# A hybrid encoder block on one core: two weight sums made by adding transfers, the first feed-forward block prepared in the output projection, the product split in weight buffers

## The chip, the cores and the metric

The kernel runs on one core of one Trainium2 chip. The metric is the device time of one execution in microseconds (us); lower is better. The engines of the core are named as the profile names them: PE (matrix products; PEld its weight loads), DVE (vector work), ACT (activations and casts), POOL (a second, slower vector engine that also issues transfers), SP (issues transfers). Each engine takes its instructions in the order in which they stand in its own list, and waits on semaphores for what other engines or transfers must have done.

## The reference, cut to what matters

```
h = concat(meta, x)                          # 16 + 512 tokens, 1024 wide
p = rmsnorm(h) @ w_in                        # q,k,v of two attention branches, two gates
o_na, o_df = neighbourhood_attention(p) @ w_na_out, diff_attention(p) @ w_diff_out
x = x + (sigmoid(g_na) * o_na + sigmoid(g_df) * o_df) @ w_o
h = rmsnorm(x)
x = x + (silu(h @ w_gate) * (h @ w_up)) @ w_down        # w_gate, w_up: 1024 x 2816
return rmsnorm(x)[16:]
```

## The kernel before, in words

All data is float32. A product of two float32 operands is made of three products of operands that are each split in a high part (a cast by ACT) and a low part (source minus high part, by DVE): `mm3` issues hi·hi, hi·lo and lo·hi. So every weight block and every activation block goes once through ACT and once through DVE before PE can use it; `split` and `wsplit` do that. Activations lie transposed (channels on the 128 partitions, tokens along the row).

The program has these stages, one behind the other. **Prologue** (`setup`): SP loads the first weight block `wraw` in two halves and the eight rows `xr` of x; ACT and DVE split the first weight block, then scale and split each row into `xh` and `xl`; POOL issues the transfers of the vector `vec` (norm weights), of `lv` (the lambda vectors, repeated over all partitions) and of `mask`. The sum of squares `ssq` of the rows is made by ACT (squares) and DVE (adds); PE forms its mean (`ms`) between the products of the third weight block. **Attention** follows, with the input projection mixed into it. **Merge** (`pn`) and **output projection** (`po`, eight blocks m = 0 to 7 of 24 products): after each block DVE adds the product to the residual `m`, and `x_operands` makes from it the operands of the feed-forward products.

**Feed-forward**: 22 blocks f of 128 columns. Gate and up products of a block are made together by a scheme of seven half-size products in place of eight: `f_products` runs the products PB11, PT1, PT4, PT2, PB21, PB22 and PT3 of 12 matmuls of 256 columns each. Its weight operands are G (the gate block, two halves), up's second half, and four sums: up0+up1 (`W[:, 1]`), up0+up1+gate0 (PT2), gate0+up0 (PT3) and the sum of all four halves (PB22). Before the change `f_load` loads G, `W[:, 0]` (up's second half) and `V[:, 0]` (up's first half) by three transfers from SP, and `f_prep` makes the sums with three adds on DVE and splits everything. `f_load` runs two blocks ahead, `f_prep` one block ahead; for block 0, `f_load(0)` stands after m = 3 of the projection and `f_prep(0)` after m = 6. The squares of x for the second norm are summed by POOL (`sum_sq`), the last one by DVE. `glu` makes g[f] from the products. **Down projection** (`pdn`): the 22 tiles g are split into `gh` and `gl`, all in one loop behind the last feed-forward block, and `d_ahead` splits the pieces of w_down into `wring`. The last of eight output blocks is done in halves (`pdh`) with the final norm behind it.

The order on each engine's list is made by a scheduler from the order of the code, priorities and estimated waits; `tc.issue_after(x)` keeps what is inside it behind instruction x on the list.

Of the kernel before, what the change touches and what calls it, by code (L numbers as in the profile page):

```python
# [71 lines left out]
class Kernel:  # L72
# [34 lines left out]
    def wsplit(self, i, parts=1, eng=None):  # L107
# [5 lines left out]
        if eng is None:  # L113
            eng = nc.gpsimd if 3 <= i < 40 and i % POOL_MOD in POOL_SET else nc.vector
        h = nk // parts
        for k in range(0, nk, h):
            nc.scalar.copy(hi[:, k:k + h], raw[:, k:k + h])  # L117
# [35 lines left out]
    def split(self, hi, lo, src):  # L153
        self.nc.scalar.copy(hi, src)  # L154
        self.nc.vector.tensor_sub(lo, src, hi.bitcast(F32))  # L155
# [49 lines left out]
    def setup(self):  # L205
# [33 lines left out]
        self.wsplit(0, 2)  # L239
        for d in self.wload(1):  # L240
            d()
        self.wemit = 2
        for k in range(KT):
            nc.scalar.activation(self.xh[:, k], xr[k], AF.Copy, scale=self.g1[:, k:k + 1])  # L244
# [974 lines left out]
```

## Time and profile before

| | |
|---|---|
| median of 3 runs | 774.57 us (773.76 to 774.62) |
| the profiled execution | 773.11 us, span 771.3 us |
| mean granted TensorE clock | 0.986 |
| PE busy | 748.6 us, 97% of the span |
| DVE, ACT, POOL busy | 575.6, 379.7, 55.3 us |
| transfers | 87.88 MB, mean 114 GB/s |

The span is the time from the first to the last instruction of the profiled execution; 1.8 us of that execution lie outside it. In rows of instructions the columns are start, duration, engine, line, operation, out<-in with its shape, and in brackets how long the engine had been idle before and what ended that. Rows by stretches give for each stretch of the span its length, the busy time of each engine with its instructions, the granted clock of PE, the busy share of the transfer engines and GB/s. Durations of matmuls overlap, so the pace of PE is read from starts or from a stretch divided by its matmuls.

### The profile page before, as it was taken

How to read it: one execution, taken by the hardware profiler on the slowest of the kernel's cores; microseconds unless marked ns; L12 is line 12 of the kernel's file. 1: busy time of each engine (PE TensorE's matmuls, PEld its weight loads, DVE VectorE, ACT ScalarE, POOL GpSimd, SP SyncE). 2: the span in 40 equal slices, each digit the busy share in tenths (PEclk: the TensorE clock that was granted, in tenths of full speed). 3: DMA queues.
4: the chain of work that ended last, by engine and by line, in shares of the span. 5: the costliest groups of instructions: out<-in, count | busy, mean ns of one | idle time of the engine just before them, and what ended most of it. 6: DMA issues, size and time to landing. Idle time of an engine off the chain costs nothing.

```text
span 771.3 us, 12598 instructions
## 1 busy us (share of the span) xinstructions
PE 748.6 (97%) x4794; PEld 674.1 (87%) x4794; DVE 575.6 (75%) x1053; ACT 379.7 (49%) x669; POOL 55.3 (7%) x141
## 2 busy tenths in 40 slices
PE   7999999999999999999998999999999989999995
PEld 5899889998889888878887999999999987888884
DVE  5777897788788867648889899999999959632214
ACT  6345545545554546514554655555555556422201
POOL 2030110110011000001121000000000000000100
PEclk8999999999999999999998999999999999999998
DMA  7474643453563412235541333333333232633003
GB/s 261 136 182 143 158 123 103 123 152 104 137 159 101 121 58 80 82 110 163 169 132 42 110 110 110 110 107 104 104 104 108 66 102 68 206 103 95 1 1 109
DMA packets 34715, 87.88 MB, mean 114 GB/s; under 512 B 4512, under 2 KB 6576, under 8 KB 34656
## 3 DMA queue, kind: packets, MB, share of 16 engines
q1 hardware_dynamic: 32688, 82.97, 35.6%
q0 software_dynamic: 1136, 3.34, 1.5%
q8 instruction: 37, 0.61, 0.3%
q10 hardware_dynamic: 832, 0.79, 0.3%
q14 instruction: 22, 0.18, 0.1%
HBM read 70.01 MB, written 2.10 MB: 93 GB/s over the span
## 4 chain that ended last, share of the span: by engine, by line
PE 85%; DVE 9%; DMA 2%; issue 1%; ACT 1%; SPq 0%; DVEq 0%; ACTq 0%
PE pdn L144 4%; PE pdn L140 4%; PE pdn L142 4%; PE pa L140 4%; PE pa L144 4%; PE pb L140 4%; PE pg L140 4%; PE pa L142 4%; PE pb L142 4%; PE pb L144 4%; PE pg L144 4%; PE pg L142 4%; PE s L513 2%; PE pv L140 2%; PE pv L142 2%; PE pv L144 2%
## 5 line engine op out<-in xcount | busy, mean ns | idle before, releaser
L117 ACT CAST whi<-wraw 128x1024 fp32r<-128x1024 f32 (+1 forms) x57 | 58.9, 1033 | 56.9 <-PE pd L142 13.1
L118 DVE TENSOR_TENSOR wlo<-wraw,whi 128x1024 fp32r<-128x1024 f32 (+1 forms) x57 | 68.5, 1201 | 17.2 <-ACT whi L117 16.9
L144 PE MATMUL pdn<-gh,wring 128*128 128x512 f32 x138 | 53.8, 390 | 1.3 <-DVE wring L155 1.3
L140 PE MATMUL pdn<-gh,wring 128*128 128x512 f32 x138 | 53.8, 390 | 0.0
L142 PE MATMUL pdn<-gl,wring 128*128 128x512 f32 x138 | 53.7, 389 | 0.0
L140 PE MATMUL pg<-xh,whi 128*128 128x512 f32 x128 | 52.6, 411 | 0.4 <-DVE vt L379 0.4
L142 PE MATMUL pg<-xl,whi 128*128 128x512 f32 x128 | 50.6, 395 | 0.0
L144 PE MATMUL pg<-xh,wlo 128*128 128x512 f32 x128 | 50.2, 393 | 0.0
L155 DVE TENSOR_TENSOR wring<-draw,wring 128x1024 fp32r<-128x1024 f32 (+1 forms) x22 | 24.7, 1126 | 28.8 <-ACT wring L154 28.8
L154 ACT CAST wring<-draw 128x1024 fp32r<-128x1024 f32 (+1 forms) x22 | 21.0, 974 | 45.9 <-PE pdn L142 34.5
L154 ACT CAST fdh<-fG 128x1024 fp32r<-128x1024 f32 x22 | 23.2, 1056 | 36.8 <-PE pa L142 34.7
L154 ACT CAST ath<-tp 128x256 fp32r<-128x256 f32 (+1 forms) x48 | 20.5, 443 | 42.2 <-PE tp L637 22.0
L1137 POOL TENSOR_TENSOR ssq<-ssq,sq 128x512 f32<-128x512 f32 x11 | 16.4, 1493 | 345.6 <-ACT sq L1136 335.2
L155 DVE TENSOR_TENSOR wlo<-fG,whi 128x1024 fp32r<-128x1024 f32 x22 | 26.9, 1224 | 14.4 <-ACT whi L154 14.4
L517 ACT ACTIVATE e<-s,m 128x528 f32<-128x528 f32 x32 | 22.5, 704 | 23.0 <-DVE m L515 22.7
L144 PEld LDWEIGHTS pdn<-gh,wring 128*128 128x128 f32 x138 | 25.9, 188 | 7.1 <-DVE wring L155 1.7
L140 PE MATMUL pk<-xh,whi 128*128 128x256 f32 (+1 forms) x128 | 28.9, 303 | 3.1 <-ACT xh L244 3.1
L140 PEld LDWEIGHTS pdn<-gh,wring 128*128 128x128 f32 x138 | 25.9, 188 | 5.6 <-ACT wring L154 0.2
L142 PEld LDWEIGHTS pdn<-gl,wring 128*128 128x128 f32 x138 | 25.9, 188 | 5.3
L155 DVE TENSOR_TENSOR fwl<-fW,fwh 128x1024 fp32r<-128x1024 f32 x22 | 26.9, 1225 | 3.1 <-ACT fwh L154 3.1
L144 PEld LDWEIGHTS pg<-xh,wlo 128*128 128x128 f32 x128 | 24.0, 188 | 5.2
L621 ACT ACTIVATE en<-en,m 128x272 f32<-128x272 f32 x32 | 16.7, 522 | 24.1 <-DVE m L619 23.8
(292 smaller groups left out, 2596.2 us busy)
## 6 DMA issues: line engine op xcount, KB each, us to landing
wraw<-in_w_in_dram SPq DMA_DIRECT2D x39, 512.0 KB, 3.8
fG<-in_w_gate_dram SPq DMA_DIRECT2D x22, 512.0 KB, 3.5
kd<-khl SPq DMA_DIRECT2D x32, 264.0 KB, 4.2
draw<-in_w_down_dram SPq DMA_DIRECT2D x16, 512.0 KB, 3.6
fW<-in_w_up_dram SPq DMA_DIRECT2D x22, 256.0 KB, 2.6
fV<-in_w_up_dram SPq DMA_DIRECT2D x22, 256.0 KB, 2.9
qs<-qhl SPq DMA_DIRECT2D x32, 128.0 KB, 2.8
wraw<-in_w_o_dram SPq DMA_DIRECT2D x8, 512.0 KB, 3.5
```

What stands on the lines that cost most here:

```text
L117: nc.scalar.copy(hi[:, k:k + h], raw[:, k:k + h])
L118: eng.tensor_tensor(out=lo[:, k:k + h], in0=raw[:, k:k + h], in1=hi[:, k:k + h].bitcast(F32), op=ALU.subtract)
L140: nc.tensor.matmul(outs[i], wh, rhs[i][0], start=start, stop=False, **kw)
L142: nc.tensor.matmul(outs[i], wh, rhs[i][1], start=False, stop=False, **kw)
L144: nc.tensor.matmul(outs[i], wl, rhs[i][0], start=False, stop=stop, **kw)
L154: self.nc.scalar.copy(hi, src)
L155: self.nc.vector.tensor_sub(lo, src, hi.bitcast(F32))
L513: nc.tensor.matmul(sc[:, r0:r1], qs[:, q], kd[:, p, r0:r1], start=p == 0, stop=p == 1)
L517: nc.scalar.activation(e, sc, AF.Exp, bias=m, accum_out=l[:, c:c + 1])
L621: x = nc.scalar.activation(e[:, :n], e[:, :n], AF.Exp, bias=m, scale=-1.0, accum_out=l[:, 0:1])
L1137: (nc.gpsimd if m < n - 1 else nc.vector).tensor_tensor(out=ssq, in0=ssq, in1=sq, op=ALU.add)
```

## The change

1. **Prologue.** `wsplit(0, 2)` becomes a generator, and the split of the second weight half moves behind rows of x. The transfers of `lv` and `mask` go from POOL's queue to SP's, behind the two transfers of `rope`.
2. **Sums by adding transfers.** `f_load` loads up0 into `W[:, 1]` and gate0 into a new tile `D[:, 0]` as well as G and `W[:, 0]`, by four transfers from SP; then POOL issues two transfers that add up1 to `W[:, 1]` and up0 to `D[:, 0]` (`accum_op=ALU.add`). `f_prep` has two adds of 512 columns left (on `D[:, 1]`) in place of two of 512 and one of 1024. Each block now moves five quarter-megabyte plain pieces in place of four, and two adding ones.
3. **Block 0 in the projection.** `f_load(0)` stands ahead of the projection, and `f_prep(0)` is spread over m = 0, 1, 2 and 6. `f_load(1)` stands after m = 5. The sums of squares go to DVE, those of m = 4 to 7 behind the last operand of x; their mean on PE moves from the third product of block 0 to its last one, PT3.
4. **Product split in weight buffers.** The pool F of feed-forward weights stays open; the tiles `gh` take its buffers (`fW`, `fD`, `fwh`, ...) as they come free. Four of the splits stand ahead of the last `glu`, four behind the first two pieces of w_down, and the rest go four by four with the products. In the last feed-forward block PB21 goes ahead of PT2.

```diff
-        self.wsplit(0, 2)
         for d in self.wload(1):
             d()
         self.wemit = 2
+        first = self.wsplit(0, 2)
         for k in range(KT):
+            if k % 3 == 0:
+                next(first, None)
             nc.scalar.activation(self.xh[:, k], xr[k], AF.Copy, scale=self.g1[:, k:k + 1])
...
-        nc.gpsimd.dma_start(lv, a["lam"].partition_broadcast(P))
+        nc.sync.dma_start(lv, a["lam"].partition_broadcast(P))
...
-        nc.gpsimd.dma_start(self.mask, a["mask"])
+        nc.sync.dma_start(self.mask, a["mask"])
...
+            self.f_load(0)
+            prep = self.f_prep(0)
             for m in range(KT):
...
-                self.x_operands(XG, xbh, xbl, xg, x1, ng2, m)
-                self.sum_sq(bt, ssq, x1[:, m], m, KT)
-                if m == 3:
-                    self.f_load(0)
-                if m == 6:
-                    self.f_prep(0)
+                x = self.x_operands(XG, xbh, xbl, xg, x1, ng2, m)
+                last_x = getattr(x, "ins", x)
+                with tc.issue_after(last_x):
+                    if m < 4:
+                        self.sum_sq(bt, ssq, x1[:, m], m, nc.vector)
+                    if m < 3 or m == 6:
+                        next(prep, None)
+                if m == 5:
                     self.f_load(1)
+
+            with tc.issue_after(last_x):
+                for m in range(4, KT):
+                    self.sum_sq(bt, ssq, x1[:, m], m, nc.vector)
...
+            def split_g(n):
+                for k in range(len(gl), min(NF, len(gl) + n)):
+                    gh.append(next(place))
+                    gl.append(G.tile([P, T], F32R, name="gl", tag="g", bufs=NF + 1))
+                    self.split(gh[k], gl[k], g[k])
...
+                if f == NF - 1:
+                    split_g(4)
                 while held:
...
             self.d_ahead(2)
+            split_g(4)
             pd = {}
-            for k in range(NF):
-                gl.append(G.tile([P, T], F32R, name="gl", tag="g", bufs=NF + 1))
-                self.split(gh[k], gl[k], g[k])
...
+                if k % 4 == 0:
+                    split_g(4)
                 block(0, k)
                 block(1, k)
...
         W = F.tile([P, 2, 4, P], F32, name="fW", tag="fW", bufs=2)
-        nc.sync.dma_start(G.rearrange("p i k n -> p (i k) n"), a["w_gate"][f])
-        nc.sync.dma_start(W[:, 0], a["w_up"][f][:, 4:8])
-        nc.sync.dma_start(V[:, 0], a["w_up"][f][:, 0:4])
+        D = F.tile([P, 2, 4, P], F32, name="fD", tag="fD", bufs=2)
+        gate, up = a["w_gate"][f], a["w_up"][f]
+        nc.sync.dma_start(W[:, 1], up[:, 0:4])
+        nc.sync.dma_start(D[:, 0], gate[:, 0:4])
+        nc.sync.dma_start(G.rearrange("p i k n -> p (i k) n"), gate)
+        nc.sync.dma_start(W[:, 0], up[:, 4:8])
+
+        nc.gpsimd.dma_start(W[:, 1], up[:, 4:8], accum_op=ALU.add)
+        nc.gpsimd.dma_start(D[:, 0], up[:, 0:4], accum_op=ALU.add)
...
-        nc.vector.tensor_tensor(out=W[:, 1], in0=V[:, 0], in1=W[:, 0], op=ALU.add)
...
-        nc.vector.tensor_tensor(out=V[:, 1], in0=W[:, 1], in1=G[:, 0], op=ALU.add)
...
-        nc.vector.tensor_tensor(out=G, in0=G, in1=V, op=ALU.add)
+        nc.vector.tensor_tensor(out=D[:, 1], in0=W[:, 1], in1=G[:, 0], op=ALU.add)
...
+        nc.vector.tensor_tensor(out=D[:, 1], in0=D[:, 1], in1=G[:, 1], op=ALU.add)
...
-                if f == 0 and i == PT4:
+                if f == 0 and i == PT3:
                     if k == 0:
                         self.ms2 = self.pj("ms2")
...
-        for part in (p2, p6, p4) if f == 0 else (p4, p6, p2):
+        for part in (p2, p6, p4) if f == 0 else (p4, p6, p2) if f < NF - 1 else (p4, p2, p6):
             part()
```

What the change moves on the engines' lists shows at three places. The first is ACT's list at the start of the program, before (`whi` is the high part of a weight block, `xh` that of a row of x):

```order
L117 CAST whi<-wraw 128x512
L244 ACTIVATE xh<-xr,vec 128x528
L117 CAST whi<-wraw 128x512
L244 ACTIVATE xh<-xr,vec 128x528 x4
L254 ACTIVATE ssq<-xr 128x528
```

The same place on ACT's list after the change:

```order
L119 CAST whi<-wraw 128x512
L250 ACTIVATE xh<-xr,vec 128x528 x2
L119 CAST whi<-wraw 128x512
L250 ACTIVATE xh<-xr,vec 128x528 x3
L260 ACTIVATE ssq<-xr 128x528
```

One row of x, not three, has moved ahead of the cast of the second weight half; DVE's list has `xl` and `wlo` in the same new order.

The second place is DVE's list from the last residual add of the projection on, before (`xt` and `xb` are the operands made from x, names with `f` are weights of the feed-forward blocks 1 and 2):

```order
L854 TENSOR_TENSOR m_3394<-m_3394,po 128x512
L155 TENSOR_TENSOR wlo<-fG,whi 128x1024
L1010 TENSOR_TENSOR xt_4611<-xg 128x256
L1137 TENSOR_TENSOR ssq_4256<-ssq_4256,sq 128x512
L155 TENSOR_TENSOR xb<-xg,xb 128x2x256
L1011 SCALAR_TENSOR_TENSOR xt_4611<-xt_4611,xg 128x256
L1044 TENSOR_TENSOR fG<-fG,fV 128x1024
L1013 SCALAR_TENSOR_TENSOR xt_4611<-xg,xt_4611 128x256
L165 TENSOR_SCALAR rs_m<-ms_4710 128x4
L1038 TENSOR_TENSOR fW<-fV,fW 128x512
L168 TENSOR_SCALAR rs_y<-rs_m 128x4
L1041 TENSOR_TENSOR fV<-fW,fG 128x512
```

The same place on DVE's list after the change:

```order
L861 TENSOR_TENSOR m_3394<-m_3394,po 128x512
L1038 TENSOR_TENSOR xt_4607<-xg 128x256
L1039 SCALAR_TENSOR_TENSOR xt_4607<-xt_4607,xg 128x256
L159 TENSOR_TENSOR xb<-xg,xb 128x2x256
L1041 SCALAR_TENSOR_TENSOR xt_4607<-xg,xt_4607 128x256
L159 TENSOR_TENSOR xb<-xt_4607,xb 128x3x256
L1174 TENSOR_TENSOR ssq_4256<-ssq_4256,sq 128x512
L159 TENSOR_TENSOR wlo<-fG,whi 128x1024
L1174 TENSOR_TENSOR ssq_4256<-ssq_4256,sq 128x512
L159 TENSOR_TENSOR fwl<-fW,fwh 128x1024
L1174 TENSOR_TENSOR ssq_4256<-ssq_4256,sq 128x512
L1075 TENSOR_TENSOR fD<-fW,fG 128x512
```

The last operands of x now follow the residual add without a break, and the split of block 1 and the sums of squares stand behind them; before, the last `xb` stood behind the mean of squares and three pieces of weight work.

The third place is DVE's list at the end of the feed-forward stage, from the sum of the last `glu` on, before:

```order
L1097 TENSOR_TENSOR s<-c_7294,pb 128x512
L1098 TENSOR_TENSOR s<-s,nR_4625 128x512
L1100 TENSOR_TENSOR u<-pa,c_7295 128x512
L1103 TENSOR_TENSOR g<-s,u 128x512
L155 TENSOR_TENSOR gl<-g,gh_7396 128x512
L155 TENSOR_TENSOR gl<-g,gh_7397 128x512
```

The same place on DVE's list after the change:

```order
L159 TENSOR_TENSOR gl<-g,gh 128x512 x4
L159 TENSOR_TENSOR dlo<-draw,dhi 128x1024
L1134 TENSOR_TENSOR s<-c_7338,pb 128x512
L1135 TENSOR_TENSOR s<-s,nR_4630 128x512
L1137 TENSOR_TENSOR u<-pa,c_7339 128x512
L1140 TENSOR_TENSOR g<-s,u 128x512
L159 TENSOR_TENSOR gl<-g,gh 128x512
L159 TENSOR_TENSOR wring<-draw,wring 128x1024
```

Four splits of g now stand ahead of the last `glu`, and the pieces of w_down (`wring`) alternate with the later ones; before, no split of g stood ahead of it.

More of the change, by code (lines that the diff above doesn't have):

```diff
@@ L114, in wsplit, with part @@
             eng = nc.gpsimd if 3 <= i < 40 and i % POOL_MOD in POOL_SET else nc.vector
+        self.wt[i] = (hi, lo)
         h = nk // parts
-        for k in range(0, nk, h):
+        def part(k):
             nc.scalar.copy(hi[:, k:k + h], raw[:, k:k + h])
@@ L119, in wsplit @@
                               op=ALU.subtract)
-        self.wt[i] = (hi, lo)
+        if parts > 1:
+            return (part(k) for k in range(0, nk, h))
+        part(0)
     def wnext(self):
@@ L866, in phase_b, with places @@
             g = []
+            gh, gl = [], []
+            def places():
+                for tag, n, bufs in (("fW", 2, 2), ("fD", 2, 2), ("fwh", 2, 2), ("fwl", 2, 2),
+                                     ("fsh", 1, 1), ("fsl", 1, 1), ("fdh", 2, 1), ("fdl", 2, 1)):
+                    for _ in range(bufs):
+                        t = self.F.tile([P, n, T], F32R, name="gh", tag=tag, bufs=bufs)
+                        for i in range(n):
+                            yield t[:, i]
+            place = places()
+            def split_g(n):
[3 more added lines that the diff above has]
+                    self.split(gh[k], gl[k], g[k])
             nR2 = G.tile([P, T], F32, name="nR2")
@@ L872, in phase_b @@
                 if f + 1 < NF:
-                    self.f_prep(f + 1)
-                held.append((f, self.f_products(G, xbh, xbl, f, ssq)))
+                    with tc.issue_after(last_x):
+                        for _ in self.f_prep(f + 1):
+                            pass
+                held.append((f, *self.f_products(G, xbh, xbl, f, ssq)))
                 if f == 0:
@@ L1004, in x_operands @@
             self.split(xbh[:, PB11, k], xbl[:, PB11, k], xg[:, m, 0])
-            self.split(xbh[:, PT1, k], xbl[:, PT1, k], t1)
-            return
+            return self.split(xbh[:, PT1, k], xbl[:, PT1, k], t1)
         self.split(xbh[:, PB21:PB22 + 1, k], xbl[:, PB21:PB22 + 1, k], xg[:, m])
@@ L1014, in x_operands @@
                                        op0=ALU.mult, op1=ALU.subtract)
-        self.split(xbh[:, PT3:PT4 + 1, k], xbl[:, PT3:PT4 + 1, k], t)
+        return self.split(xbh[:, PT3:PT4 + 1, k], xbl[:, PT3:PT4 + 1, k], t)
     def f_load(self, f):
@@ L1035, in hilo @@
             return hi, lo
-        g = hilo(G, [P, 2, 4, P], ("whi", "wlo"), 2, self.wp)
-        nc.vector.tensor_tensor(out=W[:, 1], in0=V[:, 0], in1=W[:, 0], op=ALU.add)
+        if f > 0:
+            g = hilo(G, [P, 2, 4, P], ("whi", "wlo"), 2, self.wp)
         w = hilo(W, [P, 2, 4, P], ("fwh", "fwl"), 2, F)
-        nc.vector.tensor_tensor(out=V[:, 1], in0=W[:, 1], in1=G[:, 0], op=ALU.add)
-        s = hilo(V[:, 1], [P, 4, P], ("fsh", "fsl"), 1, F)
-        nc.vector.tensor_tensor(out=G, in0=G, in1=V, op=ALU.add)
-        d = hilo(G, [P, 2, 4, P], ("fdh", "fdl"), 1, F)
+        yield
+        nc.vector.tensor_tensor(out=D[:, 1], in0=W[:, 1], in1=G[:, 0], op=ALU.add)
+        s = hilo(D[:, 1], [P, 4, P], ("fsh", "fsl"), 1, F)
+        yield
+        nc.vector.tensor_tensor(out=D[:, 1], in0=D[:, 1], in1=G[:, 1], op=ALU.add)
+        d = hilo(D, [P, 2, 4, P], ("fdh", "fdl"), 1, F)
+        yield
+        if f == 0:
+            g = hilo(G, [P, 2, 4, P], ("whi", "wlo"), 2, self.wp)
         p = lambda t, i: (t[0][:, i], t[1][:, i])
@@ L1127, in d_ahead, with sum_sq @@
             self.dsplit += 1
-    def sum_sq(self, bt, ssq, x, m, n):
+    def sum_sq(self, bt, ssq, x, m, eng=None):
         nc = self.nc
@@ L1136, in sum_sq @@
             nc.scalar.activation(sq, x, AF.Square)
-            (nc.gpsimd if m < n - 1 else nc.vector).tensor_tensor(out=ssq, in0=ssq, in1=sq, op=ALU.add)
+            (eng or nc.gpsimd).tensor_tensor(out=ssq, in0=ssq, in1=sq, op=ALU.add)
 _INS = ["x", "vec", "lam", "w_in", "rope", "mask", "rpb", "w_df", "w_na", "w_o", "w_gate", "w_up", "w_down"]
```

19 lines of the change are left out of this document (6 added, 13 removed).

## The prediction

> **What bounds the kernel now.** I read the busy times first, then the waits of PE, then the busy times by stretch with the borders put where PE's stages meet.
>
> ```profile
> PE 748.6 (97%) x4794; PEld 674.1 (87%) x4794; DVE 575.6 (75%) x1053; ACT 379.7 (49%) x669; POOL 55.3 (7%) x141
> ...
> 0.00:18.50 18.50, 13.97 (x54) 10.63 (x55) 10.32 (x15) 11.80 (x18) 5.17 (x30) 0.82 0.79 270
> 36.00:341.00 305.00, 304.94 (x1879) 269.30 (x1878) 238.86 (x591) 156.62 (x323) 29.45 (x92) 1.00 0.43 121
> 364.60:408.10 43.50, 43.50 (x193) 36.03 (x192) 36.57 (x50) 25.76 (x40) 8.25 (x9) 1.00 0.44 141
> 408.10:422.70 14.60, 10.81 (x63) 10.17 (x63) 14.29 (x29) 6.40 (x10) 2.30 (x1) 0.77 0.18 55
> 422.70:632.90 210.20, 210.20 (x1797) 209.72 (x1797) 184.58 (x230) 119.12 (x193) 0.00 (x0) 1.00 0.32 102
> 632.90:650.00 17.10, 13.45 (x58) 10.24 (x57) 15.20 (x23) 14.72 (x26) 0.00 (x0) 1.00 0.08 23
> 650.00:742.40 92.40, 92.40 (x410) 76.47 (x409) 33.88 (x38) 26.39 (x31) 6.95 (x5) 1.00 0.33 99
> ```
>
> PE is the bound in the attention (304.94 of 305 us), in the projection (43.5 of 43.5), in the feed-forward blocks (210.2 of 210.2, so 210.2 / 1797 = 0.117 us a matmul, 84 x 0.117 = 9.83 us a block) and in the down projection (92.4 / 410 = 0.225 us a matmul). DVE has 184.58 / 210.2 = 88% in the blocks and is not the bound. Time can be won at three seams alone: the first 18.5 us, the entry to the feed-forward blocks (63 matmuls in 14.6 us; at 0.117 us they take 7.4, so 7.2 us are lost) and the entry to the down projection (58 in 17.1 us; at 0.225 us 13.1, so 4.0 us are lost). The waits at these seams:
>
> ```profile
> PE pk L140 <- ACT xh L244: 3.1, 1, 3.1
> PE ms L181 <- DVE ssq L1137: 2.2, 1, 2.2
> PE pdn L142 <- DVE gl L155: 1.6, 1, 1.6
> PE pdn L144 <- DVE wring L155: 1.3, 1, 1.3
> PE pc L140 <- ACT xb L154: 0.9, 1, 0.9
> PE pc L142 <- DVE xb L155: 0.8, 1, 0.8
> PE pdn L140 <- ACT gh L154: 0.7, 1, 0.7
> ```
>
> 2.2 + 0.9 + 0.8 = 3.9 us of the second seam are waits; the rest goes with the lower granted clock in the same row, 0.77. At the third seam 1.6 + 1.3 + 0.7 = 3.6 of 4.0 us are waits.
>
> **The change, part by part. Prologue.** The second half of the first weight block and the software queue (q0, POOL's transfers) in the microsecond from 6 to 7:
>
> ```profile
> 2.13 0.43 SPq L104 DMA_DIRECT2D wraw<-in_w_in_dram  x1
> ...
> 9.13 0.62 ACT L117 CAST whi<-wraw 128x512 fp32r<-128x512 f32 x1 [3.52 <-DMA wraw<-in_w_in_dram]
> ...
> 10.44 0.81 PE L140 MATMUL pk<-xh,whi 128*128 128x256 f32 x2 [3.07 <-ACT xh L244]
> ...
> q0 software_dynamic: 19, 0.06, 63.2%
> q1 hardware_dynamic: 30, 0.06, 26.7%
> ...
> 22.27 0.70 DVE L258 TENSOR_TENSOR ssq<-ssq,sq 128x528 f32<-128x528 f32 x1
> ...
> 25.60 0.75 PE ms L181 x8
> ```
>
> ACT waits 3.52 us for the half weight block, issued at 2.13, and row 1 of x stands behind it on ACT's list; PE therefore stops 3.07 us and runs on at a reduced clock (0.82 in the stretch). POOL's small transfers hold 63% of the transfer engines there for 0.06 MB, as little as SP's queue then moves. Two edits meet this: one row of x goes ahead of the cast, and `lv` and `mask` go behind x and the first two weight blocks. If the half block still lands at 9.13, only one row's work is out of the way: a cast of 0.62 us and its share of PE's work, 0.7 us won. If it lands when `lv` and `mask` no longer stand between, some 2 to 2.5 us earlier, the stop of 3.07 us nearly goes and the clock recovers earlier: up to 4 us. The sum of squares, the next thing late, ends at 22.97 and PE asks for it at 25.60, so 2.6 us of PE's advance are free of it, and its own chain moves up with the rows. The moved transfers cost the same engine time in SP's queue ahead of the third weight block, which has 512 KB to land before its use some 8 us later: nothing, up to 1 us if late. I take 2.5, nearer to the second end because the q0 row names the cause; ends 0.7 and 4.0.
>
> **Entry to the feed-forward blocks.** DVE and ACT rows there (start, duration):
>
> ```profile
> 413.67 0.68 DVE L854 TENSOR_TENSOR m<-m,po 128x512 f32<-128x512 f32 x1
> ...
> 414.38 0.72 ACT L998 ACTIVATE xg<-m,ng 128x512 f32<-128x512 f32 x1 [0.82 <-DVE m L854]
> ...
> 415.40 0.42 DVE L1010 TENSOR_TENSOR xt<-xg 128x256 f32<-128x256 f32 x1
> ...
> 418.86 0.83 ACT L154 CAST xb<-xt 128x768 fp32r<-128x768 f32 x1 [2.73 <-DVE xt L1013]
> ...
> 412.80 0.95 DVE L155 TENSOR_TENSOR xb<-xt,xb 128x768 fp32r<-128x768 f32 x1
> ...
> 414.26 1.22 DVE L155 TENSOR_TENSOR wlo<-fG,whi 128x1024 fp32r<-128x1024 f32 x1
> ...
> 415.73 0.69 DVE L1137 TENSOR_TENSOR ssq<-ssq,sq 128x512 f32<-128x512 f32 x1
> ```
>
> The last `po` ends at 408.1, but DVE is so far behind that its add starts at 413.67 and the last cast of `xb` at 418.86. Two things put it behind: the preparation of block 0, and POOL's adds:
>
> ```profile
> 379.69 1.30 POOL L1137 TENSOR_TENSOR ssq<-ssq,sq 128x512 f32<-128x512 f32 x1 [10.40 <-issue]
> ...
> 379.76 1.51 DVE L1003 TENSOR_TENSOR xt<-xg 128x256 f32<-128x256 f32 x1
> ...
> 383.84 0.42 DVE L1003 TENSOR_TENSOR xt<-xg 128x256 f32<-128x256 f32 x1
> ```
>
> The same DVE operation takes 1.51 us beside POOL's add and 0.42 without: POOL's six adds cost DVE about 1.1 us each, 6.5 in all; on DVE itself an add costs 0.69. After the change the chain from the last `po` is 0.68 + 0.72 + 3 x 0.42 + 0.83 + 0.95 = 4.4 us, so the last operand stands at 412.6. PE has 24 matmuls of PB11 and PT1 and 9 of PT4 without it, 33 x 0.117 = 3.9 us, to 412.0: a wait of 0.6 us. Behind it DVE makes four adds, two splits and one sum, 5 x 0.69 + 2 x 1.22 = 5.9 us, to 418.5; PE reaches the mean in PT3 44 matmuls later, at 412.6 + 5.1 = 417.7: 0.8 us more at most. Block 1's weights are split by then and PE is served. Of 7.2 us lost, 6.0 come back. Ends: 7.0 with no wait, 3.5 if the waits cost the clock again as they do now.
>
> **Adding transfers.** No row shows one. The nearest are plain transfers from POOL and SP, and the load of the queues in the projection (340 to 420 us) and in the blocks (440 to 600):
>
> ```profile
> 349.12 0.55 POOL L840 DMA_DIRECT2D m<-in_x_dram  x1 [109.32 <-DVE ml L155]
> ...
> m<-in_x_dram POOLq DMA_DIRECT2D x8, 256.0 KB, 3.1
> ...
> fW<-in_w_up_dram SPq DMA_DIRECT2D x4, 256.0 KB, 3.1
> ...
> q0 software_dynamic: 640, 2.10, 8.7%
> ...
> q1 hardware_dynamic: 7180, 17.48, 33.4%
> ...
> L1044 DVE TENSOR_TENSOR fG<-fG,fV 128x1024 f32<-128x1024 f32 x20 | 24.4, 1218 | 0.0
> ```
>
> POOL's transfer of 256 KB lands in 3.1 us, as SP's does, and costs the engines 0.087 x 80 / 2.10 = 3.3 us per MB against 0.334 x 160 / 17.48 = 3.1. A block now moves four pieces of 256 KB at 33.4%, 8.35% a piece. Five plain pieces make 42%, two adding ones 17% if an addition costs nothing, 33% if it costs as much as a second transfer: 59 to 75% of the engines, so PE still sets the pace. POOL waits for SP's load and issues in order, 2 x 0.55 us a block, with nothing queued behind; the tile is loaded two blocks ahead and used one block ahead, so a landing of even 10 us is covered. If that cover went, DVE would stop at `fD` or `fwl`, and with it `glu`. DVE saves 1.22 + 2 x 0.69 - 2 x 0.69 = 1.2 us a block, worth nothing beside a full PE. Only block 0 is tight: its first sum can land some 375.5 (loads from 366.8, about 4.5 us, then an addition of 4), ACT and DVE wait for it with the next w_o split queued behind, and PE wants that at 380.9 with 2.4 us of work ahead: 3 us of slack, cost nothing, up to 2 us.
>
> The Trainium skill (SBUF — State Buffer, section "SBUF: two separate sides") says that a vector operation in a two-port mode keeps GpSimd from writing descriptors, so that a transfer from its queue starts late: 620 ns become 3100 in its example. By it each addition would land 2.5 us later, an estimate; the sum would be the same but for block 0. In this trace POOL's issue takes 0.55 us and lands in 3.1 beside a DVE that is 84% busy, so no such delay shows for these operations.
>
> **Entry to the down projection.**
>
> ```profile
> 633.23 1.14 ACT L154 CAST gh<-g 128x512 fp32r<-128x512 f32 x2 [1.86 <-DVE s L1097]
> ...
> 635.53 12.56 DVE L155 TENSOR_TENSOR gl<-g,gh 128x512 fp32r<-128x512 f32 x16
> ```
>
> All splits of g stand behind the last `glu`; then 16 run in one piece of 12.56 us and the first `wring` waits behind them. After the change four pairs are ready, and each serves 2 x 3 x 0.225 = 1.35 us of PE, 5.4 us together, while DVE needs about 2.5 us for the last `glu` and then 0.69 + 1.22 for one split and one piece. Of 4.0 us, 3.8 come back; ends 2.5 and 4.0.
>
> **Sum.** 2.5 + 6.0 + 3.8 = 12.3 us. Against the profiled execution's 773.1 that is 760.8; it lies 1.5 under the median of 774.6, so the median comes to 762.3. Best ends: 4.0 + 7.0 + 4.0 = 15.0, 759.6. Worst: 0.7 + 3.5 + 2.5 less 2 for block 0 = 4.7, 769.9.
>
> **Rivals.** (a) The seams give only part: the half weight block lands as late as now and PE's clock falls again at the second seam. For it speaks that a wait of 2.2 us there now brings the clock to 0.77; against it that only about 1.4 us of waits are left. 774.6 - (0.7 + 3.5 + 3.8) = 766.6. (b) Slower: adding transfers are so dear that the transfer engines become the bound. Five plain pieces leave 58% for two additions; the point is 29% each, 3.5 times a plain piece. At 4 times the load is 109%, and 21 blocks of 9.83 us lose 9% = 18.6 us: 762.3 + 18.6 = 781. For it: an addition reads two sources and no row has its price; against it: POOL's plain transfer is only 1.08 times as dear as SP's. (c) The two cancel: additions a little over the point, near 774.6. (d) POOL's descriptor writing blocks DVE as its adds do: 2 x 1.1 us a block, on 8.6 - 1.2, is 9.6 of 9.83 us, so the blocks hold and only the entry suffers, 1 to 2 us: 764. Against it, DVE rows beside POOL's issues keep 0.69.
>
> **How the numbers follow.** Full gain with its ends (759.6 to 765) 0.60; (a) 0.15 and (d) 0.08, both faster; (b) 0.12; (c) 0.05. Faster 0.83, within 0.2% (1.5 us, about what a measurement can tell) 0.05, slower 0.12. The range leaves out (b), (c) and little more: 758.5 to 769.
>
> **What would show it.** Prologue: the cast of the second half starts before 7.5 and `ms` before 23.5; if it still starts near 9, the q0 reading is wrong. Second seam: the last `xb` split starts within 5 us of the last `po`, and the stretch from there holds its clock above 0.9. Blocks: PE full, transfer engines at 60 to 75%, additions landing under 6 us; a wait of PE for `fwh`, `fsh` or `fdh` in mid-stage would be (b). Third seam: no wait of `pdn` above 0.5 us. DVE's share in the blocks falls to about 75%. Wrong it is above all if an addition costs much more than two transfers.

## The result, and the profile after

The changed kernel takes 768.75 us (median of 4 runs, 767.71 to 769.92); the kernel before, run beside it, 774.16 us. The ratio is 0.9935, with a 95% interval of 0.9912 to 0.9958: 5.4 us less, where 12.3 were forecast. The profiled execution took 769.92 us with a span of 768.1, against 771.3 before. It is the slowest of the four, and the profiled one of the kernel before (773.11) lay about 1 us below its median, so the traces show 3.2 of the 5.4 us.

The stages are cut where PE starts the first matmul of the next one. The rows of four tiles in the trace after give the cuts; the columns are the count, the shortest, median and longest matmul in ns, and the first and the last start in us.

```profile
L144 PE MATMUL po<-mh,whi x64: 389/389/628, 361.4 to 408.0; 128*128 128x512 f32 x64
...
L144 PE MATMUL pa<-xb,whi x88: 277/280/1202, 408.7 to 625.3; 128*128 128x256 f32 x88
...
L144 PE MATMUL pdn<-gh,dhi x16: 389/389/398, 634.0 to 644.3; 128*128 128x512 f32 x16
...
L144 PE MATMUL pdh<-gh,wring x44: 278/283/365, 738.8 to 756.7; 128*128 128x256 f32 x44
```

From these, and from the same rows of every other trace, come the lengths below (us). "To projection" is everything ahead of the first `po`; "projection" runs to the first `pa`, "blocks" to the first `pdn`, "down" to the first `pdh`, "rest" to the end. The ratio of times, with its 95% interval, is to the kernel before, run on the same chip. The kernels e1 to e12 are the experiments further down.

| kernel | to projection | projection | blocks | down | rest | span | median | ratio (95%) |
|---|---|---|---|---|---|---|---|---|
| before | 364.6 | 43.5 | 225.8 | 108.5 | 28.9 | 771.3 | 774.16 | |
| after | 361.4 | 47.3 | 225.3 | 104.8 | 29.3 | 768.1 | 768.75 | 0.9935 (0.9912 to 0.9958) |
| e1 sums on DVE | 361.6 | 43.5 | 233.6 | 104.8 | 29.3 | 772.8 | 776.35 | 1.0044 (1.0028 to 1.0060) |
| e2 block 0 on DVE | 361.4 | 45.7 | 231.4 | 104.8 | 29.4 | 772.7 | 767.66 | 0.9942 (0.9921 to 0.9962) |
| e3 block 0 one later | 361.7 | 45.9 | 225.9 | 104.8 | 29.3 | 767.6 | 768.69 | 0.9947 (0.9928 to 0.9965) |
| e4 means first | 361.4 | 46.4 | 225.3 | 104.8 | 28.4 | 766.3 | 768.99 | 0.9945 (0.9920 to 0.9969) |
| e5 small on POOL | 364.1 | 46.2 | 224.0 | 104.8 | 29.1 | 768.2 | 771.92 | 0.9992 (0.9976 to 1.0009) |
| e6 rows old order | 362.4 | 46.0 | 225.4 | 104.8 | 29.3 | 767.9 | 768.49 | 0.9947 (0.9933 to 0.9962) |
| e7 splits in one | 362.1 | 47.3 | 225.4 | 108.6 | 29.3 | 772.7 | 773.13 | 1.0002 (0.9988 to 1.0016) |
| e8 casts bound | 361.6 | 44.2 | 223.1 | 104.7 | 28.5 | 762.1 | 763.85 | 0.9896 (0.9880 to 0.9913) |
| e9 squares early | 362.4 | 46.6 | 223.9 | 104.7 | 29.0 | 766.6 | 767.28 | 0.9938 (0.9924 to 0.9953) |
| e10 three together | 361.8 | 46.1 | 219.3 | 104.8 | 28.4 | 760.4 | 762.35 | 0.9873 (0.9858 to 0.9888) |
| e11 gate cast free | 361.4 | 43.5 | 223.5 | 104.7 | 28.5 | 761.6 | 764.64 | 0.9893 (0.9867 to 0.9918) |
| e12 sums apart | 361.6 | 48.1 | 227.0 | 104.7 | 29.3 | 770.7 | 772.81 | 0.9997 (0.9985 to 1.0008) |

The change won 3.2 us ahead of the projection and 3.7 in the down projection. It lost 3.8 us in the projection, which had been full before, and won 0.5 of the 6.0 us forecast for the blocks' entry; 0.4 more went at the end. PE's waits in these stages say where (in all, times, longest, us); before, PE had none in the projection and none for `rp` in the blocks:

```profile
PE rp L915 <- DVE dg L191: 2.3, 1, 2.3
...
PE po L148 <- DVE wlo L120: 1.6, 1, 1.6
...
PE pa L148 <- DVE wlo L159: 1.2, 1, 1.2
...
PE pc L146 <- DVE xb L159: 0.6, 1, 0.6
...
PE pc L144 <- ACT xb L158: 0.4, 1, 0.4
```

The busy times in the stretches used before (length, then PE, PEld, DVE, ACT and POOL busy with counts, granted clock, share of the transfer engines, GB/s):

```profile
0.00:18.50 18.50, 15.28 (x68) 10.59 (x69) 12.52 (x18) 14.62 (x23) 4.18 (x28) 1.00 0.86 300
...
364.60:408.10 43.50, 41.85 (x177) 33.91 (x176) 29.65 (x49) 25.20 (x39) 5.86 (x7) 0.96 0.66 187
408.10:422.70 14.60, 12.32 (x97) 11.43 (x95) 12.48 (x18) 7.94 (x13) 0.00 (x0) 1.00 0.18 61
422.70:632.90 210.20, 207.76 (x1758) 206.32 (x1759) 168.98 (x225) 123.33 (x206) 33.28 (x38) 0.99 0.69 173
632.90:650.00 17.10, 17.10 (x83) 14.33 (x82) 16.12 (x21) 9.48 (x13) 0.00 (x0) 1.00 0.58 167
```

The first 18.5 us hold 68 matmuls instead of 54, the entry 97 instead of 63, and the down projection's start is full. But the projection's stretch holds 177 instead of 193, and the blocks' stretch has 2.4 us in which PE is idle, where it had none.

**The projection.** SP and POOL issue block 0's loads and additions early, and ACT's cast of the sum then stands and waits, with DVE behind it:

```profile
363.61 0.33 SPq L1053 DMA_DIRECT2D fW<-in_w_up_dram  x1
...
367.45 0.92 POOL L1058 DMA_DIRECT2D fW<-in_w_up_dram  x1 [1.35 <-PE po L148]
...
375.48 1.05 ACT L158 CAST fwh<-fW 128x1024 fp32r<-128x1024 f32 x1 [6.09 <-DMA fW<-in_w_up_dram]
...
376.87 0.43 DVE L159 TENSOR_TENSOR xb<-xt,xb 128x256 fp32r<-128x256 f32 x1 [6.99 <-ACT xb L158]
...
380.22 0.50 PE L148 MATMUL po<-mh,wlo 128*128 128x512 f32 x1 [1.65 <-DVE wlo L120]
...
372.00:376.00 4.00, 4.00 (x20) 3.30 (x19) 0.00 (x0) 0.52 (x1) 1.72 (x2) 1.00 1.08 271
...
380.00:384.00 4.00, 3.78 (x10) 3.01 (x11) 3.04 (x7) 2.30 (x5) 0.00 (x0) 0.61 0.44 133
```

From 372 to 376 DVE does nothing at all, and the transfer engines are full (the share adds up packet times, so it can pass 1). The row order on ACT is `xb`, `fwh`, `xb`, then the next w_o cast: a wait at the head of ACT's list holds everything behind it. PE waits 1.65 us for the w_o split, and then runs at a granted clock of 0.61, with matmuls 0.43 us apart instead of 0.227. By their starts the matmuls behind the wait, from 380.2 to 384.4, lose 1.7 us by this; the rest of the 3.8 us are a few longer steps around the wait.

**The entry to the blocks.** The mean's small operations on DVE (`rs_m` is the first, `dg` spreads their result, and PE uses it in `rp`), after; then before:

```profile
420.30 0.33 SPq L1053 DMA_DIRECT2D fW<-in_w_up_dram  x1
...
422.84 0.16 DVE L169 TENSOR_SCALAR rs_m<-ms 128x4 f32<-128x4 f32 x1 [0.23 <-PE ms L185]
...
423.60 0.88 POOL L1058 DMA_DIRECT2D fW<-in_w_up_dram  x1 [28.35 <-DVE fD L1079]
...
429.22 0.69 DVE L1075 TENSOR_TENSOR fD<-fW,fG 128x512 f32<-128x512 f32 x1 [1.55 <-DMA fW<-in_w_up_dram]
...
434.69 0.69 DVE L191 TENSOR_TENSOR dg<-ident,rs_y 128x512 f32<-128x512 f32 x1
...
435.43 2.06 PE L915 MATMUL rp<-dg,ones 128*128 128x512 f32 x2 [2.32 <-DVE dg L191]
...
436.00:438.00 2.00, 2.00 (x6) 1.06 (x5) 1.11 (x1) 0.48 (x1) 0.84 (x1) 0.50 1.06 278
```

```profile
418.74 0.16 DVE L165 TENSOR_SCALAR rs_m<-ms 128x4 f32<-128x4 f32 x1
...
422.99 0.69 DVE L187 TENSOR_TENSOR dg<-ident,rs_y 128x512 f32<-128x512 f32 x1
...
L882 PE MATMUL rp<-dg,ones x2: 590/590/591, 436.2 to 436.6; 128*128 128x512 f32 x2
```

Before, 12 small operations and the spreading product `dg` started 4.3 us apart from first to last. After, it is 11.9 us, since the preparation of the next blocks stands between them, one piece of it waiting for an adding transfer. Before, PE came to `rp` at 436.2, 12.5 us after `dg` was done, and had no wait there. After, it comes to `rp` at 433.1, where `dg` ends at 435.4: the operations start 4.1 us later and take 7.6 us longer, and PE is 3.1 us earlier, which uses up the 12.5 us and 2.3 more. The clock falls to 0.50 behind the wait.

**The blocks.** The same 120 us of before and after, then the queues and POOL's issues of the changed kernel between 440 and 600 us:

```profile
480.00:600.00 120.00, 120.00 (x1031) 120.00 (x1030) 109.04 (x136) 69.07 (x112) 0.00 (x0) 1.00 0.34 110
```

```profile
480.00:600.00 120.00, 120.00 (x1031) 120.00 (x1030) 96.78 (x122) 67.15 (x110) 21.04 (x24) 1.00 0.76 190
...
q1 hardware_dynamic: 9149, 20.86, 41.3%
q0 software_dynamic: 4699, 8.56, 32.2%
...
fD<-in_w_up_dram POOLq DMA_DIRECT2D x16, 256.0 KB, 7.3
fW<-in_w_up_dram POOLq DMA_DIRECT2D x16, 256.0 KB, 6.1
```

PE issues 1031 matmuls in both, so a block takes 9.8 us as before. In the 160 us of the queue rows, 32 additions hold the transfer engines for 0.322 x 160 / 32 = 1.61 us each; 80 plain pieces of 256 KB (20.86 MB) for 0.413 x 160 / 80 = 0.83. An adding transfer costs 1.95 plain ones, and DVE falls from 91 to 81%.

### The profile page after: what moved, and what is told of

It reads as the page before. It is cut to its first block, busy times and chain, and to the rows that moved or that the text cites. A ratio compares the mean times of both kernels' runs of the same rounds, so it can differ in the third digit from the quotient of the medians.

```text
span 768.1 us, 12721 instructions
## 1 busy us (share of the span) xinstructions
PE 747.4 (97%) x4794; PEld 671.0 (87%) x4794; DVE 551.0 (72%) x1037; ACT 378.2 (49%) x669; POOL 83.5 (11%) x177
## 4 chain that ended last, share of the span: by engine, by line
PE 86%; DVE 7%; DMA 3%; ACT 2%; issue 2%; SPq 0%; DVEq 0%; POOL 0%; ACTq 0%
PE pdn L148 5%; PE pdn L144 5%; PE pdn L146 5%; PE pg L144 4%; PE pa L144 4%; PE pg L148 4%; PE pg L146 4%; PE pa L148 4%; PE pa L146 4%; PE pb L146 4%; PE pb L148 4%; PE pb L144 4%; PE s L519 2%; PE pv L144 2%; PE pv L146 2%; PE pv L148 2%
## 5 line engine op out<-in xcount | busy, mean ns | idle before, releaser
L158 ACT CAST wring<-draw 128x1024 fp32r<-128x1024 f32 (+1 forms) x22 | 21.0, 974 | 50.9 <-PE pdn L146 46.2
L158 ACT CAST fdh<-fD 128x1024 fp32r<-128x1024 f32 x22 | 23.2, 1054 | 34.8 <-PE pa L146 32.3
L158 ACT CAST fwh<-fW 128x1024 fp32r<-128x1024 f32 x22 | 23.1, 1049 | 24.0 <-PE pc L146 14.8
L1059 POOL DMA_DIRECT2D fD<-in_w_up_dram x22 | 19.5, 887 | 123.1 <-DVE fsl L159 49.9
L941 DVE TENSOR_TENSOR t<-pdn,nR 128x512 f32<-128x512 f32 x7 | 4.8, 691 | 34.0 <-PE pdn L148 34.0
```

The lines of the kernel that those rows point to most:

```text
L941: nc.vector.tensor_tensor(out=t, in0=pd[m], in1=nR2, op=ALU.mult)
L1059: nc.gpsimd.dma_start(D[:, 0], up[:, 0:4], accum_op=ALU.add)
```

## The experiments

Each starts from the changed kernel unless it says otherwise.

**e1, all sums on DVE; e2, block 0's alone.** `up[0:4]` is loaded into `D[:, 0]`, nothing adds on the way, and `f_prep` makes both sums on DVE. The cut shows e1; e2 has the same under `if f == 0`.

```
-        nc.sync.dma_start(W[:, 1], up[:, 0:4])
-        nc.sync.dma_start(D[:, 0], gate[:, 0:4])
+        nc.sync.dma_start(D[:, 0], up[:, 0:4])
...
-        nc.gpsimd.dma_start(W[:, 1], up[:, 4:8], accum_op=ALU.add)
-        nc.gpsimd.dma_start(D[:, 0], up[:, 0:4], accum_op=ALU.add)
...
+        nc.vector.tensor_tensor(out=W[:, 1], in0=D[:, 0], in1=W[:, 0], op=ALU.add)
...
+        nc.vector.tensor_tensor(out=D[:, 0], in0=D[:, 0], in1=G[:, 0], op=ALU.add)
```

> The changed kernel, but all 22 blocks make the two sums with DVE adds of 0.69 us and no transfer adds. Yardsticks in the changed kernel: 47.3 us from the first matmul of the output projection to the first of the blocks (43.5 before), 225.3 us from there to the first of the down projection (225.8 before). Theory 1 (the first adding transfer of block 0 is late and holds ACT, and DVE behind it, in the projection): the projection falls to 43.5 to 44 us, 3.8 less. Rival 2 (the early loads of blocks 0 and 1 crowd the w_o weights out, whatever kind they are): 46 to 47 us stay. Theory 3 (PE's 2.3 us wait for the row of means comes from the preparation of block 3 that waits for its adding transfer in the queues of ACT and DVE): that wait falls below 0.8 us and the blocks to about 221 us. Rival 4 (DVE is simply too full there): the wait stays at 2 us or grows, 225 to 227 us. DVE's share in the blocks rises from about 80 to 91%, PE stays full. Time: 761 if 1 and 3 hold, 765 with 1 and 4, 769 with 2 and 4.

> The changed kernel, but block 0 alone makes its two sums with DVE adds; the other 21 keep the adding transfers. Theory 1: the projection falls from 47.3 to 43.5 to 44 us and the time to about 765. Rival 2 (the early loads crowd the w_o weights out): 46 to 47 us, time 767.5 to 768.7. The wait for the row of means, 2.3 us, stays by either.

Without any addition in it (e1) the projection takes 43.5 us again, as theory 1 has it. With block 0's alone gone (e2) it takes 45.7, since ACT now meets block 1's sum, which it also casts in the projection:

```profile
376.90 1.05 ACT L158 CAST fwh<-fW 128x1024 fp32r<-128x1024 f32 x1 [4.80 <-DMA fW<-in_w_up_dram]
```

That miss sharpens the theory: what counts is any adding transfer at the head of ACT's list there, not block 0's. e1's blocks were 8.3 us longer, and its row of means waited 3.5 us; neither was expected in this size. There DVE's first sum waits for the load into the fD buffer, which is free last:

```profile
480.36 0.69 DVE L1069 TENSOR_TENSOR fW<-fD,fW 128x512 f32<-128x512 f32 x1 [2.64 <-DMA fD<-in_w_up_dram]
...
492.82 0.39 PE L144 MATMUL pa<-xb,fdh 128*128 128x256 f32 x1 [2.34 <-ACT c L1117]
```

So e1's blocks can't be taken as the price of the adding transfers. e2's median (767.66) gives nothing clear of the changed kernel either, where theory 1 had 765. e2's profile is of the slowest of its ten runs (774.46), with fewer matmuls per us all through the blocks at a granted clock of 1.00; why is not known, and only its projection is read here.

**e3, block 0's steps one projection product later.**

```
-                    if m < 3 or m == 6:
+                    if 1 <= m < 4 or m == 6:
                         next(prep, None)
```

> The changed kernel, but the three steps of block 0's preparation stand one projection product (5.4 us) later; the adding transfers are all kept. Theory 1: the first sum landed at 375.4 and would now be asked for about 5 us after the 369.4 of the changed kernel, so at most 1 us of waiting on ACT is left, the projection falls to 43.5 to 44 us, time about 765. Rival 2: 46 to 47 us stay, time 767.5 to 768.7. The entry to the blocks is the same or up to 1 us longer, since the third step ends later.

45.9 us and an unchanged time: theory 1 as written failed. The edit orders DVE alone; ACT's cast kept its place and waited as long as before:

```profile
375.54 1.05 ACT L158 CAST fwh<-fW 128x1024 fp32r<-128x1024 f32 x1 [5.92 <-DMA fW<-in_w_up_dram]
```

**e8, the same bound on ACT too.** The casts of block 0's steps stand behind the last cast of `xb`, two products later, and block 1's behind the very last. `last_c` is ACT's latest cast of `xb` at that point.

```
-                    if m < 3 or m == 6:
-                        next(prep, None)
+                    if 2 <= m < 5 or m == 6:
+                        with tc.issue_after(last_c):
+                            next(prep, None)
...
-                    with tc.issue_after(last_x):
+                    with tc.issue_after(last_x), tc.issue_after(last_c):
                         for _ in self.f_prep(f + 1):
```

> The changed kernel with all adding transfers, but the three steps of block 0's preparation stand two products later on ACT as well as on DVE, and block 1's casts stand behind the last cast of xb. Theory 1b (ACT's list is what blocks: its cast of block 0's sums stood ahead of the next w_o cast and waited 5.5 to 6.1 us for the adding transfer; the edit before this moved DVE alone): no wait of ACT for an adding transfer above 1 us in the projection, which takes 43.5 to 44.2 us; time about 765. Rival 2 (the transfer engines are full there, and the w_o weights themselves land late): 45.5 to 47 us, time 767.5 to 768.7. The wait for the row of means stays near 2.3 us by both.

The projection takes 44.2 us and the kernel 763.85, with every adding transfer in place. ACT's cast starts without a wait, at 380.90; in e11 further down, which keeps the bindings of the three sums, it starts at 380.66, PE is full, and the transfer engines are as busy as ever. e8's row, then e11's:

```profile
380.90 1.04 ACT L158 CAST fwh<-fW 128x1024 fp32r<-128x1024 f32 x1
...
380.66 1.05 ACT L158 CAST fwh<-fW 128x1024 fp32r<-128x1024 f32 x1
...
370.00:375.00 5.00, 5.00 (x24) 4.14 (x23) 2.75 (x5) 2.59 (x5) 1.04 (x2) 1.00 1.05 288
375.00:380.00 5.00, 5.00 (x24) 4.14 (x23) 3.17 (x6) 2.65 (x5) 0.71 (x1) 1.00 1.10 302
```

Rival 2, full transfer engines, is out: they are full here, and nothing is lost. That the wait for the means also went was not expected; less stands between the small operations there (8.1 us from the first to `dg`), probably because block 1's casts moved. So part of e8's gain lies in the blocks (223.1 us).

**e4, the means ahead of block 3's preparation on DVE.** `dg_last` is the product that makes `dg`.

```
-                    with tc.issue_after(last_x):
+                    with tc.issue_after(dg_last if f >= 2 else last_x):
                         for _ in self.f_prep(f + 1):
```

> The changed kernel, but DVE's part of the preparation of blocks 3 and later stands behind the product that spreads the means (dg). Theory 3 (the means wait behind block 3's preparation, which waits for its adding transfer): dg ends by 432, PE's wait of 2.3 us goes and with it the lowered clock behind it, 42 matmuls of 0.117 us: 4.8 us less, the blocks take 220.5 us, time about 764. Rival 4 (moving the sum of squares to DVE and the mean to the last product has used up the cover, whatever stands between): the wait stays above 1 us, time 767 to 768.7. The projection stays at 47.3 us by both.

PE's wait for `dg` went, as theory 3 says, and the blocks still took 225.3 us: the stall came back two blocks later, where DVE stood 3.95 us ahead of the first use of a sum whose addition POOL had issued at 446.15. ("issue" marks a wait whose releaser the trace doesn't name; ACT's cast of the same sum starts in the same instant, at 451.47, so the addition's landing is the likely one.)

```profile
451.48 0.69 DVE L1076 TENSOR_TENSOR fD<-fW,fG 128x512 f32<-128x512 f32 x1 [3.95 <-issue]
...
453.63 0.39 PE L144 MATMUL pa<-xb,fdh 128*128 128x256 f32 x1 [2.06 <-ACT c L1119]
```

**e9, three of the last four adds of squares back in the projection's loop.**

```
-                    if m < 4:
+                    if m < KT - 1:
                         self.sum_sq(bt, ssq, x1[:, m], m, nc.vector)
...
-                for m in range(4, KT):
-                    self.sum_sq(bt, ssq, x1[:, m], m, nc.vector)
+                self.sum_sq(bt, ssq, x1[:, KT - 1], KT - 1, nc.vector)
```

> The changed kernel, but three of the four last adds of the sum of squares go back into the projection's loop (on DVE), so only the last one, 0.69 us, stands behind the last operand. Theory 5 (the mean starts 3 x 0.69 = 2.1 us late, and then its 12 small operations are threaded between the preparation of blocks 2 and 3): ms starts near 419 instead of 421.0, dg ends about 2 us earlier, PE's wait of 2.3 us nearly goes, 2 to 4 us less: 765 to 767. Rival 6 (DVE's work is only moved: the last operands of xb come later by as much, or dg still waits behind the adding transfer of block 3): blocks at 224.5 to 226 us, time 768 to 769.

The wait for `dg` went, but not for the reason given: the small operations began at 426.30, later than the 422.84 of the changed kernel, because the adds now stand ahead of the last operands. PE met its waits earlier instead (1.8 us for block 0's split, 1.3 for `xb`). The ratio is the same within its interval, so in time DVE's work was only moved, as rival 6 has it.

**e10, e8 and e9 with blocks 2 and later behind `dg`; e11, the same with block 0's gate cast unbound.** Beside the two diffs above, first e10's line, then e11's:

```
+                    with tc.issue_after(dg_last if f >= 1 else last_x), tc.issue_after(last_c):
...
-                    if 2 <= m < 5 or m == 6:
+                    if 2 <= m < 5:
                         with tc.issue_after(last_c):
                             next(prep, None)
+                    if m == 6:
+                        next(prep, None)
```

> The last two edits together, and DVE's part of the preparation of blocks 2 and later behind dg. If theories 1b and 5 both hold and no later stall takes their place: projection 43.5 to 44.2, PE's wait for the row of means below 0.5 us, blocks 220 to 221 us, 768.75 - 3.5 - 4.8 = 760.5. If an adding transfer that is issued later holds up block 4 or 5, as it did when block 3's preparation alone was moved (a wait of 2.1 us and a lowered clock behind it): blocks 224 to 226, time 764 to 765.

> The three edits together (762.35, projection 46.1 us with a wait of 2.4 us ahead of the first block matmul), but the cast of block 0's gate weights is no longer bound behind the last-but-one cast of xb on ACT. If that binding makes the wait: the cast starts by 403, the wait falls below 0.5 us, the projection takes 43.6 to 44.2 us, time 760.2 to 760.8. If the weights' own landing or DVE's split makes it, the wait stays at 1.5 to 2.5 us and the time at 762.

e10 has the lowest median here: 762.35 us, 0.9873 (0.9858 to 0.9888) of before. `dg` comes 4.1 us after the first small operation, PE has no wait for it, and the blocks take 219.3 us. DVE still stands 2.1 us ahead of a sum, until 436.38, but PE does not wait there. e10's projection is longer by a wait for the gate weights of block 0, whose cast starts late on ACT:

```profile
407.90 0.36 PE L144 MATMUL pa<-xb,whi 128*128 128x256 f32 x1 [2.42 <-issue]
...
406.76 1.04 ACT L158 CAST whi<-fG 128x1024 fp32r<-128x1024 f32 x1
```

e11 takes that wait away (cast at 399.43, projection 43.5) and is no faster: PE reaches the blocks 3 us earlier and waits 1.2 us for the split of the gate weights and 1.3 and 0.6 for the last `xb`. From the first `po` to the first `pdn` e10 takes 265.4 us and e11 267.0, before 269.3 and after 272.6. What ends the entry by then is DVE's last operands.

**e5, `lv` and `mask` back on POOL's queue; e6, ACT's old order of rows.** e5's lines, then e6's:

```
-        nc.sync.dma_start(lv, a["lam"].partition_broadcast(P))
+        nc.gpsimd.dma_start(lv, a["lam"].partition_broadcast(P))
...
-        nc.sync.dma_start(self.mask, a["mask"])
+        nc.gpsimd.dma_start(self.mask, a["mask"])
...
-            if k % 3 == 0:
-                next(first, None)
+            if k == 0:
+                for _ in first:
+                    pass
```

> The changed kernel, but lv and mask go by POOL's queue as before. In the changed kernel the second half of the first weight block is cast at 6.98 us and the first matmul of the output projection starts at 361.4 (9.13 and 364.6 before). Theory P1 (those small transfers hold the engines while the second half waits): the cast goes back to 8.5 to 9.2, the projection starts at 363 to 364, time 770 to 771. Rival P2 (issuing the half block after two rows of x and putting rows ahead of the cast did it): 6.9 to 7.2 and 361.4 to 361.8 stay, time 768.7.

> The changed kernel (lv and mask on SP's queue), but ACT casts the second half of the first weight block behind one row of x, as before, not two. The run with lv and mask back on POOL lost the whole prologue gain (cast at 9.45, projection from 364.1). Theory P1 (the queue alone counts): the half block lands before 7 anyway, cast at 5.8 to 6.6 or as soon as it lands, the projection starts at 361.0 to 361.8, time 768.2 to 769. Rival P3 (both edits are needed: ACT again waits for the half block with the second row behind it): a wait of PE for xh of 0.5 to 1.5 us, projection from 362 to 363, time 769.5 to 770.5.

e5 loses 2.7 of the prologue's 3.2 us (the projection starts at 364.1), though the new order of rows stands. The first row is of the changed kernel, the others are of e5:

```profile
6.98 0.62 ACT L119 CAST whi<-wraw 128x512 fp32r<-128x512 f32 x1
...
9.45 0.62 ACT L119 CAST whi<-wraw 128x512 fp32r<-128x512 f32 x1 [3.23 <-DMA wraw<-in_w_in_dram]
...
q0 software_dynamic: 22, 0.07, 63.4%
...
10.90 0.51 PE L144 MATMUL pk<-xh,whi 128*128 128x256 f32 x2 [2.93 <-ACT xh L250]
```

e6 gives a wait of 1.1 us and starts the projection 1.0 us later, as P3 has it, but its ratio (0.9947) can't be told from 0.9935. So the queue made most of the gain; the row order is worth about 1 us in the traces and nothing that the times can tell.

**e7, all products split in one piece behind the last block.**

```
-                if f == NF - 1:
-                    split_g(4)
...
             self.d_ahead(2)
-            split_g(4)
+            split_g(NF)
```

> The changed kernel, but all 22 products g are split in one piece behind the last block, as before (they still lie in the weight buffers). From the first matmul of the down projection to the first of its last output half the changed kernel takes 104.8 us, before 108.5. If the four pairs that are ready early are the whole of it, 108 to 108.6 us and time 772 to 772.5, with waits of PE for gl and wring above 2.5 us together. Rival (the order of the last block's products, which was changed too, gives part of it): 106 to 107.5 us, time 770 to 771.5.

The down projection is back at 108.6 us and the kernel at 773.13, so the order of the splits is the whole of that gain, and the new order of the last block's products has no part in it. The edit takes away both the four early pairs and the later ones' spreading, so the two are not told apart. The waits are less than was expected: there is one, of 2.0 us. The matmuls from 638.7 to 641.7 then come 0.43 us apart, which makes most of the rest:

```profile
637.40 0.50 PE L146 MATMUL pdn<-gl,dhi 128*128 128x512 f32 x1 [1.99 <-DVE gl L159]
```

**e12, e10 with both sums on DVE and a buffer of their own for `up[0:4]`.** The second fD buffer makes the room.

```
+        V = F.tile([P, 4, P], F32, name="fV", tag="fV", bufs=2)
+        nc.sync.dma_start(V, up[:, 0:4])
...
+        nc.vector.tensor_tensor(out=W[:, 1], in0=V, in1=W[:, 0], op=ALU.add)
...
+        nc.vector.tensor_tensor(out=D[:, 0], in0=V, in1=G[:, 0], op=ALU.add)
```

> The three edits together (762.35), but no transfer adds: the second half of the up weights has a buffer of its own again (room from the second fD buffer), and DVE makes both sums, 2 x 0.69 us a block. The earlier run with the sums on DVE built the first sum on the fD buffer, which is the last to come free (DVE waited 0.6 to 2.6 us a block for that load), so its slow blocks (233.6 us) don't price the adding transfers. If adding transfers buy nothing but DVE time that lies beside a full PE: a block stays at 9.80 us, the stretch from the first matmul of the projection to the first of the down projection takes 265 to 268 us (265.4 with the adding transfers), time 762 to 765. If DVE's slack (it needs some 8.0 us of 9.8 a block with them, 9.4 without) is what lets the blocks catch up behind the entry: waits of PE for c or for weights in blocks 2 to 6, 270 us or more, time 767 or more.

772.81 us, so the second case by its time. PE waits 4.4 us ahead of the first block and loses 34 matmuls in the 120 us below; DVE waits for the loads of its new buffer (16.0 us in 12 waits between 440 and 620). Some of the 34 are of another kind: where PE is full, from 480 to 520, it issues 172 in 20 us, not 174, and why is not known.

```profile
480.00:600.00 120.00, 118.76 (x997) 117.40 (x996) 105.94 (x144) 64.19 (x106) 0.00 (x0) 1.00 0.32 106
...
DVE fW L1072 <- DMA fV<-in_w_up_dram: 16.0, 12, 2.0
```

The kernel before has DVE busier still (109.04 of 120) with PE full, so DVE's share alone isn't the cause. That its buffers and order are is likely and not shown. How much the adding transfers are worth in themselves stays open: no run here has both kinds with equally early loads.

## Why the prediction was right and wrong, point by point

- **Prologue, 2.5 (0.7 to 4.0).** 3.2 us. The half block's cast starts at 6.98, the q0 reading was right, and e5 shows it. `ms` starts at 22.47 against 25.60, within the 23.5 given as its mark.
- **Down entry, 3.8.** 3.7 us, no wait of `pdn`; e7 shows it.
- **Adding transfers in the blocks, 0.** Right for the blocks once they run evenly: 9.8 us a block, PE full, engines at 76% where 59 to 75% was said. The cover that the step counted on was missing at the entry: block 3's load was issued at 420.30, right behind the last use of its buffer, its addition at 423.60, and it landed at 429.2, while DVE asked at 427.7 and stood 1.55 us. Two marks missed: additions land in 6.1 and 7.3 us, not under 6, and DVE is at 81%, not 75%. Rival (b) needed 3.5 plain pieces for one addition; it is 1.95.
- **Block 0, cost nothing, up to 2.** The mis-sized term: 3.8 us. The mechanism was the one named, ACT and DVE waiting with the w_o split behind them. The landing came out right (375.5; ACT's wait ends at 375.48) by luck: the loads were issued 3.2 us earlier than assumed, and the addition took 8.0 us from its issue at 367.45, not 4, with the engines full (1.08 of 1 between 372 and 376). PE, 3.2 us ahead, wanted its w_o split that much sooner. So the 3 us of slack were gone, a wait of 1.65 us came, and the price of the lowered clock behind it, about 1.7 us, was not in the step at all.
- **Entry to the blocks, 6.0 (3.5 to 7.0).** The step that failed: 0.5 us came back. (Its own terms, 7.2 less 0.6 and 0.8, give 5.8.) The two causes named for DVE's lateness were real, and the stretch to 422.7 holds 97 matmuls at a clock of 1.00, though the last `xb` split starts 5.9 us behind the last `po`, where 5 was the mark. But the step ended at the mean. It followed neither the 12 small operations on DVE nor `rp` behind them: these lost their clear stretch to the preparation of the next blocks, and a wait of 2.3 us and a clock of 0.50 came one block later. Of the entry's own waits, 1.2 us fell on a split that the change puts last (block 0's gate weights), for which the step had no row; the same split, 409.30 to 410.43, kept DVE from the residual add behind the last `po`. With the chain cleared the blocks do take 6.5 us less (e10, 219.3 against 225.8), but 2.6 of that came back as a longer projection.
- **Rivals.** 768.75 lies nearest to (a) in time, but not by its mechanism: the half block is early, and the clock fell at two other places. (d): DVE's splits beside POOL's issues keep their 1.22 us and POOL's issues take 0.87 to 1.14 us, so none is held up by more than about 0.3 us. The delay of 2.5 us, the prediction's estimate from the Trainium skill (SBUF — State Buffer, section "SBUF: two separate sides"), shows in no issue; in the landing it can't be told from the queue.
- **Sum.** By the traces: 3.2 + 3.7 + 0.5 - 3.8 - 0.4 = 3.2 us. The projection varied from trace to trace of kernels that have the same code there (46.0 to 47.3 us with e4, e5, e6 and e7), which may be part of what lies between 3.2 and the medians' 5.4.

## What to carry to other kernels

A wait at the head of an engine's list costs what stands behind it, so where a transfer is made slower (here 1.95 times), move its first reader down the list on every engine that reads it: ordering DVE alone, one product later, won nothing, and ordering ACT as well, two products later, took 3.1 us out of the projection and 3.0 us off the time by the ratios (0.9896 against 0.9935). When a seam is cleared, follow the chain to the last operation that PE needs from it, small ones too, and ask what the freed engine will put between them. And price a new wait of PE with the clock that may follow it: here a wait of 1.65 us stood in a loss of 3.8.

## What the runs showed of the hardware

An adding transfer of 256 KB from a queue of POOL holds the transfer engines 1.61 us against 0.83 for a plain one, takes some 0.87 us to issue against 0.54, and lands in 6.1 to 7.3 us (medians of its two kinds) when the engines are 76% busy.

PE's clock fell to half behind waits of 1.65 and 2.3 us, and of 2.0 us in e7, for about 3 us each: matmuls 0.43 us apart at 382 to 384, a granted clock of 0.50 at 436 to 438. The Trainium skill (TensorE: Matmul & The Clock Gate, section "What's actually happening") has the clock halve after an idle window of about 3.4 us; these waits are shorter, so the trace does not agree with that as a bound. Nor does every wait do it: the three waits of 0.7 to 1.6 us at the old down entry left the clock at 1.00, and so did e10's wait of 2.4 us ahead of its first block (matmuls 0.117 us apart from 408.1 on), longer than any of the three that were followed by half clock. So the length of one wait doesn't decide it here, and what does stays open.
